# A decoder layer on one core: a new beginning ahead of the first projection chunk

## The chip, the core and the metric

The kernel runs on one core of one Trainium2 chip. A core has engines with queues of their own: TensorE (PE in the profile; its weight loads are PEld), VectorE (DVE), ScalarE (ACT), GpSimd (POOL) and SyncE (SP), which here only issues loads. Each engine works through its instructions in order and waits on semaphores for the others. The metric is the device time of one execution in microseconds (us).

## The reference, cut to what matters

A vector `c` of 2048 numbers modulates a layer on 256 tokens of width 2048. Everything is float32.

```python
c_act = jax.nn.silu(c)
mod = (c_act @ w_mod[l] + b_mod[l])[:, None, :]
sh_m, sc_m, g_m, sh_f, sc_f, g_f = jnp.split(mod, 6, axis=-1)
h = rmsnorm(x, mix_pre_w[l]) * (1 + sc_m) + sh_m
y = hybrid_mixer(h, w_in[l], ...)      # starts with proj = h @ w_in, 2048 x 6160
x = x + g_m * rmsnorm(y, mix_post_w[l])
# then the same with sh_f, sc_f, g_f around a causal ConvFFN
```

So before the first product with `w_in` there have to be: the norm of `x`, and those columns of `sh_m` and `sc_m` that belong to the first part of the width.

## The kernel before, in words

**Chunks and units.** The projection `h @ w_in` runs over the width in four chunks of 2, 4, 5 and 5 tiles of 128 (`CHUNKS`). Only the modulation of the first chunk (256 columns of `sh_m` and of `sc_m`) has to be there before TensorE starts; that of chunk 1 is summed while chunk 0 runs, and so on. A chunk has 12 units or more (`in_units`); one of chunk 0 loads a block of `w_in` of 256 x 512 (512 KB) into a `raw` buffer (`prep`), of which there are `NRAW = 6`, all shared with the rows of `w_mod`.

**High and low parts.** A weight and an activation are each split into a high part, rounded to fp32r by ScalarE (`high`: `wh`; for activations `act_high`), and a low part, the rest, by VectorE (`low`: `wl`; `act_low`). TensorE adds three products: high by high, high by low, low by high. A unit of chunk 0 is 8 triples, 24 matmuls of 256 columns.

**The modulation.** Row `j` of `w_mod` (one of 16 per partition) is scaled by `c_act[:, j]` and added to an accumulator by VectorE (`mod_steps`, `stt`). The sum over partitions is a product with ones on TensorE (`mod_columns`), of which two VectorE instructions make the columns `ash` (shift, and one plus scale times the norm's weight). Such a float32 product with two columns is two passes on TensorE.

**The beginning** (lines 957 to 979). The 16 rows are summed on VectorE. After row 3 the norm of token half 0 stands in its queue, after row 14 that of half 1: squares on ScalarE (`norm_squares`), a reduction, a square root on ScalarE, a reciprocal, and the scaling, of the first 256 columns on VectorE and of the rest on ScalarE. TensorE transposes the scaled tiles into PSUM (`turn_norm`), multiplies the accumulator with ones, and ScalarE writes the modulated tiles `hf` to SBUF, then their high parts.

**What sets the order.** The program text sets each engine's order: `drive` calls, for each unit, the preparation of later units, its own matmuls and the steps hung on it (`early`, `mid`, `late`). SP issues loads in the order of the text; each waits for a free buffer, so for the instruction that used the buffer last. In chunk 0 SP's order is two units, a pair of `w_mod` rows (two loads), a unit, a pair, two units, and so on. The fifth unit's load takes the buffer of the first unit's, which the first low part gives back.

## Time and profile before

| what | value |
|---|---|
| median of 3 runs | 1223.4 us (1222.33 to 1223.87) |
| the profiled execution | 1223.4 us, its span 1221.5 us |
| PE busy | 1174.3 us, 96% of the span |
| DVE busy | 955.2 us, 78% |
| ACT busy | 572.9 us, 47% |
| mean over the span | 263 GB/s |
| first column copy (`ash`) | 26.35 us |
| first low part of a weight | 29.62 us |
| first matmul of chunk 1 | 76.54 us |

The span runs from the first to the last instruction; the rest of the profiled execution lies around it. "Busy" counts an engine that holds an instruction, and the ends of matmuls are modelled. A wait is put down to what ended last. The granted clock of TensorE is shown as 1.00 wherever the profile holds no record of it; the first record begins at 36.4 us, so what the clock was before has to be read from the distance of the matmuls.

### The profile page before, as it was taken

How to read it: one execution, taken by the hardware profiler on the slowest of the kernel's cores; microseconds unless marked ns; L12 is line 12 of the kernel's file. 1: busy time of each engine (PE TensorE's matmuls, PEld its weight loads, DVE VectorE, ACT ScalarE, POOL GpSimd, SP SyncE). 2: the span in 40 equal slices, each digit the busy share in tenths (PEclk: the TensorE clock that was granted, in tenths of full speed). 3: DMA queues.
4: the chain of work that ended last, by engine and by line, in shares of the span. 5: the costliest groups of instructions: out<-in, count | busy, mean ns of one | idle time of the engine just before them, and what ended most of it. 6: DMA issues, size and time to landing. Idle time of an engine off the chain costs nothing.

```text
span 1221.5 us, 17082 instructions
## 1 busy us (share of the span) xinstructions
PE 1174.3 (96%) x6977; PEld 1043.0 (85%) x6977; DVE 955.2 (78%) x973; ACT 572.9 (47%) x668; POOL 31.7 (3%) x49
## 2 busy tenths in 40 slices
PE   2999999999999998999999999999999999999997
PEld 1999999989997787888888888888888888888885
DVE  5999999989998879974787979798885665444464
ACT  5553432443565437444554555454545543433441
POOL 2000020000001001000000000000000000000000
PEclk9999999999999998998999999999999999999999
DMA  9999999987599995995575776758664665555522
GB/s 306 386 390 385 311 358 394 397 284 254 190 324 347 336 343 205 383 360 169 180 268 202 250 277 208 275 206 278 239 234 150 249 246 189 207 178 201 195 81 69
DMA packets 128046, 320.73 MB, mean 263 GB/s; under 512 B 8341, under 2 KB 35685, under 8 KB 118240
## 3 DMA queue, kind: packets, MB, share of 16 engines
q1 hardware_dynamic: 125360, 312.63, 71.9%
q0 software_dynamic: 2320, 6.94, 1.6%
q8 instruction: 55, 0.90, 0.3%
q14 instruction: 23, 0.19, 0.0%
q10 hardware_dynamic: 288, 0.07, 0.0%
HBM read 315.42 MB, written 4.19 MB: 262 GB/s over the span
## 4 chain that ended last, share of the span: by engine, by line
PE 54%; DVE 0%; ACT 0%; DVEq 0%; issue 0%; ACTq 0%
PE ps L874 22%; PE ps L876 11%; PE ps L733 7%; PE ps L734 7%; PE ps L732 7%; PE ps L285 0%; DVE big L137 0%; PE ps L348 0%; PE ps L308 0%; PE ps L309 0%; ACT junk L335 0%; DVE big L727 0%; DVEq L1234 0%; DVE big L799 0%; ACT rz L321 0%
## 5 line engine op out<-in xcount | busy, mean ns | idle before, releaser
L141 ACT CAST wh<-raw 128x2048 fp32r<-128x2048 f32 (+3 forms) x202 | 366.2, 1816 | 500.2 <-PE ps L874 163.5
L146 DVE TENSOR_TENSOR wl<-raw,wh 128x2048 fp32r<-128x2048 f32 (+3 forms) x202 | 437.7, 2168 | 137.1 <-ACT wh L141 137.1
L874 PE MATMUL ps<-big,wh 128*128 128x512 f32 x1400 | 490.2, 394 | 0.0
L876 PE MATMUL ps<-big,wl 128*128 128x256 f32 x1400 | 393.3, 281 | 0.0
L874 PEld LDWEIGHTS ps<-big,wh 128*128 128x128 f32 x1400 | 263.4, 188 | 59.3
L876 PEld LDWEIGHTS ps<-big,wl 128*128 128x128 f32 x1400 | 265.8, 190 | 0.0
L479 PE MATMUL ps<-big,wl 128*128 128x256 f32 x733 | 210.7, 287 | 4.6 <-DVE wl L146 4.6
L477 PE MATMUL ps<-big,wh 128*128 128x256 f32 x733 | 211.9, 289 | 0.2 <-ACT wh L141 0.2
L478 PE MATMUL ps<-big,wh 128*128 128x256 f32 x733 | 209.9, 286 | 0.0
L137 DVE SCALAR_TENSOR_TENSOR macc<-raw,c_act,macc 128x2048 f32<-128x2048 f32 (+1 forms) x96 | 199.4, 2077 | 3.7 <-DMA raw<-in_w_mod_dram 3.6
L733 PE MATMUL ps<-wl,big 128*128 128x512 f32 x456 | 177.8, 390 | 3.6 <-DVE wl L146 3.6
L732 PE MATMUL ps<-wh,big 128*128 128x512 f32 x456 | 177.9, 390 | 0.0
L734 PE MATMUL ps<-wh,big 128*128 128x512 f32 x456 | 177.5, 389 | 0.0
L479 PEld LDWEIGHTS ps<-big,wl 128*128 128x128 f32 x733 | 143.1, 195 | 5.8 <-DVE wl L146 5.7
L477 PEld LDWEIGHTS ps<-big,wh 128*128 128x128 f32 x733 | 143.4, 196 | 2.7 <-PE ps L423 1.3
L478 PEld LDWEIGHTS ps<-big,wh 128*128 128x128 f32 x733 | 143.3, 196 | 0.1
L733 PEld LDWEIGHTS ps<-wl,big 128*128 128x128 f32 x456 | 85.6, 188 | 22.4 <-DVE wl L146 4.8
L732 PEld LDWEIGHTS ps<-wh,big 128*128 128x128 f32 x456 | 85.6, 188 | 17.8
L734 PEld LDWEIGHTS ps<-wh,big 128*128 128x128 f32 x456 | 85.6, 188 | 17.6
L137 DVE SCALAR_TENSOR_TENSOR big<-big,fcw,big 128x254 f32<-128x254 f32 (+1 forms) x176 | 72.2, 479 | 0.0
L799 DVE TENSOR_TENSOR big<-big,ps 128x256 f32<-128x256 f32 x88 | 31.1, 416 | 43.5 <-ACT big L797 43.5
L819 ACT ACTIVATE big<-big,fcw 128x256 f32<-128x256 f32 x88 | 37.8, 512 | 14.1 <-DVE big L810 14.1
(183 smaller groups left out, 686.9 us busy)
## 6 DMA issues: line engine op xcount, KB each, us to landing
raw<-in_w_up_dram SPq DMA_DIRECT2D x88, 1024.0 KB, 5.3
raw<-in_w_mod_dram SPq DMA_DIRECT2D x64, 1024.0 KB, 7.1
raw<-in_w_down_dram SPq DMA_DIRECT2D x44, 1024.0 KB, 4.8
raw<-in_w_in_dram SPq DMA_DIRECT2D x24, 960.0 KB, 8.3
raw<-in_w_mod_dram SPq DMA_DIRECT2D x32, 640.0 KB, 7.8
raw<-in_w_out_dram SPq DMA_DIRECT2D x16, 1024.0 KB, 7.0
raw<-in_w_in_dram SPq DMA_DIRECT2D x12, 1024.0 KB, 8.0
raw<-in_w_mod_dram SPq DMA_DIRECT2D x22, 512.0 KB, 6.7
```

Of the source, the lines that this page charges most:

```text
L137: nc.vector.scalar_tensor_tensor(o, a, s, b, op0=op0, op1=op1)
L141: nc.scalar.copy(hi, raw)
L146: nc.vector.tensor_sub(lo, raw, hi.bitcast(F32))
L477: nc.tensor.matmul(ps, w[0][:, kk, cs], ht[:, k % 2, 0, :], start=st, stop=False)
L478: nc.tensor.matmul(ps, w[0][:, kk, cs], ht[:, k % 2, 1, :], start=False, stop=False)
L479: nc.tensor.matmul(ps, w[1][:, kk, cs], ht[:, k % 2, 0, :], start=False, stop=sp)
L732: nc.tensor.matmul(ps, a[:, i, 0, ts_], w[0][:, kk, ns], start=st, stop=False)
L733: nc.tensor.matmul(ps, a[:, i, 0, ts_], w[1][:, kk, ns], start=False, stop=False)
L734: nc.tensor.matmul(ps, a[:, i, 1, ts_], w[0][:, kk, ns], start=False, stop=sp)
L819: nc.scalar.activation(st["c"][:, o, :], st["u"][o], AF.Copy, scale=fcw[:, 2, ch + o:ch + o + 1])
L874: nc.tensor.matmul(pss[o], wh[:, kk, cs], h2[k // 2][:, k % 2, :, :], start=(first and kk == 0), stop=False)
L876: nc.tensor.matmul(pss[o][:, 1, :], wl[:, kk, cs], h2[k // 2][:, k % 2, 0, :], start=False, stop=(last and kk == 3))
```

## The change

Six things are changed, all in the beginning.

- Twelve of the first chunk's 16 rows are summed on VectorE as before. The last four (12 to 15) are loaded into `big` slots and multiplied on TensorE with two columns of `c_act` (`first_products`): four float32 products a row, added in PSUM to the four products of ones with the accumulator. `c_act` gets two columns of zeros at its end, so that row 15 has a second column.
- The loads of the second half of `x` move ahead of rows 8 to 11. The norm of half 0 stands after row 5 in VectorE's queue, that of half 1 after row 9; the squares of half 0 are issued ahead of all rows.
- TensorE gets 16 and later 8 products of ones, 128 x 128 by 128 x 512 (`keep_busy`), whose result nothing reads.
- The high part of the first chunk's activations is written by ScalarE straight from PSUM, while VectorE writes `hf` from PSUM (`at_once`).
- The first unit runs its products in three passes (high by high, low weight by high, high by low), and the chunk's product with `alr_w` and its copy come behind it.
- The small loads move: the identity and the first bias stand first on POOL's queue, `alr_w` behind the first two units on SP's, and the casts of ones go from ScalarE to VectorE.

TensorE's queue from the start to the first unit (`ident`: transposes; `sv_r`: small vectors; `ones`: the sum of an accumulator; `alr_w`: gate rank; `wh`, `wl`: weights of the unit). Before:

```order
L209 MATMUL ps_184<-ident,sv_r 128x58
L348 MATMUL ps_187<-ident,big_109 128x128 x2
L348 MATMUL ps_187<-ident,big_149 128x128 x2
L285 MATMUL ps_193<-ones,big_102 128x2 x4
L423 MATMUL ps_204<-big_99,alr_w 16x256 x2
L477 MATMUL ps_232<-big_202,wh_211 128x256
L478 MATMUL ps_232<-big_202,wh_211 128x256
L479 MATMUL ps_232<-big_202,wl_213 128x256
```

The same place in the changed kernel:

```order
L229 MATMUL ps_182<-ident,sv_r 128x58
L368 MATMUL ps_185<-ident,big_111 128x128 x2
L217 MATMUL ps_188<-big_88,ones_r 128x512 x16
L1040 MATMUL ps_206<-c_act,big_125 128x2 x8
L1040 MATMUL ps_206<-ones,big_79 128x2 x4
L217 MATMUL ps_219<-big_88,ones_r 128x512 x8
L368 MATMUL ps_185<-ident,big_118 128x128 x2
L1040 MATMUL ps_206<-c_act,big_128 128x2 x8
L510 MATMUL ps_270<-big_244,wh_240 128x256 x2
```

Between the first transposes and the sum now stand 16 products of ones and the eight of rows 12 and 13; the second transposes stand behind eight more of ones, and the eight products of rows 14 and 15 are the last before the columns.

VectorE's queue from the accumulator's bias to the scaling of half 0 (`n_...`: sums and reciprocals of the norm; `c_act`: a row's step). Before:

```order
L187 TENSOR_TENSOR big_102<-big_102,big_103 1x512
L319 TENSOR_REDUCE n_12_130<-n_7_121 128x1
L326 RECIPROCAL n_13_132<-n_13_132 128x1
L967 TENSOR_SCALAR big_109<-big_109,n_13_132 128x256
L137 SCALAR_TENSOR_TENSOR big_102<-raw_138,c_act,big_102 128x512 x4
```

And now:

```order
L201 TENSOR_TENSOR big_79<-big_79,big_80 1x512
L136 SCALAR_TENSOR_TENSOR big_79<-raw_115,c_act,big_79 128x512 x2
L339 TENSOR_REDUCE n_19_151<-n_14_135 128x1
L346 RECIPROCAL n_20_153<-n_20_153 128x1
L1008 TENSOR_SCALAR big_111<-big_111,n_20_153 128x256
L136 SCALAR_TENSOR_TENSOR big_79<-raw_115,c_act,big_79 128x512 x2
```

Rows 4 and 5 now stand ahead of the norm's reduction.

VectorE's queue from the columns (`ash`) to the third low part of a weight. Before:

```order
L288 COPY ash_192<-ps_193 128x2
L137 SCALAR_TENSOR_TENSOR ash_192<-ps_193,sv 128x2
L367 TENSOR_TENSOR big_202<-big_99,big_202 128x2x256
L431 COPY alr<-ps_204 16x256
L146 TENSOR_TENSOR wl_213<-raw_209,wh_211 128x1024
L137 SCALAR_TENSOR_TENSOR big_219<-raw_222,c_act,big_219 128x1024
L146 TENSOR_TENSOR wl_230<-raw_215,wh_217 128x1024
```

And now:

```order
L1052 COPY ash_205<-ps_206 128x2
L136 SCALAR_TENSOR_TENSOR ash_205<-ps_206,sv 128x2
L440 TENSOR_SCALAR big_105<-ps_185,ash_205 128x256 x2
L387 TENSOR_TENSOR big_244<-big_105,big_244 128x2x256
L145 TENSOR_TENSOR wl_250<-raw_238,wh_240 128x1024
L136 SCALAR_TENSOR_TENSOR big_257<-raw_260,c_act,big_257 128x1024
L145 TENSOR_TENSOR wl_268<-raw_252,wh_254 128x1024
L136 SCALAR_TENSOR_TENSOR big_257<-raw_260,c_act,big_257 128x1024
L469 COPY alr<-ps_296 16x256
```

Two instructions that read PSUM are new ahead of the activations' low part, and the copy `alr` went behind the second low part.

The diff, cut to its core:

```diff
--- before.py
+++ after.py
@@ -35,8 +35,8 @@
 LWS = 1
 ORD = (0, 5, 1, 6, 2, 7, 3, 8, 4, 9, 10)
 NBIG = 20
-XLD = (0, 8)
-NLD = (3, 14)
+XLD = (0, 4)
+NLD = (5, 9)
 GATE = (18, 19, 20, 21)
 SILU = (17, 18)
 CONV = (9, 12, 13, 15)
@@ -49,6 +49,8 @@
 NHI = 3
 NLO = 3
 NHF = 3
+ROWS = 12
+BUSY = (16, 8)
...
@@ -70,9 +72,6 @@
 def drive(units):
     due = {}
     n = len(units)
-    units[0].prep()
-    units[0].low()
-    units[1].prep()
     for i, u in enumerate(units):
         for f in u.early:
             f()
@@ -149,13 +148,14 @@
 
     c_sb = col(KT, "c_sb")
     nc.scalar.dma_start(c_sb, c.rearrange("b (p j) -> p (b j)", j=KT))
-    c_act = col(KT, "c_act")
-    nc.scalar.activation(c_act, c_sb, AF.Silu)
+    c_act = col(KT + 2, "c_act")
+    nc.vector.memset(c_act, 0.0)
+    nc.scalar.activation(c_act[:, :KT], c_sb, AF.Silu)
 
...
+    W0 = CHUNKS[0] * P
+    first_acc = slot([P, 2, W0])
+    first_b = slot([1, 2, W0])
+    first_rows = {}
+
+    def first_load(j, m, tile):
+        r = tile([P, m, 2, W0])
+        for s in range(2):
+            nc.sync.dma_start(r[:, :, s, :], w_mod_v[:, j:j + m, s, 0:W0])
+        for i in range(m):
+            first_rows[j + i] = r[:, i, :, :]
+
+    def first_step(j):
+
+        cj = c_act[:, j:j + 1]
+        if j == 0:
+            nc.vector.tensor_scalar_mul(first_acc, first_rows[j], cj)
+        else:
+            stt(first_acc, first_rows[j], cj, first_acc)
+        if j == 3:
+            nc.vector.tensor_add(first_acc[0:1], first_acc[0:1], first_b)
 
     ident = col(P, "ident")
-    nc.scalar.dma_start(ident, ident_in)
+    nc.gpsimd.dma_start(ident, ident_in)
+    nc.gpsimd.dma_start(first_b, b_mod_v[:, 0:2, 0:W0])
     ones = col(P, "ones")
     nc.gpsimd.memset(ones, 1.0)
     ones_r = col(P, "ones_r", F32R)
-    nc.scalar.copy(ones_r, ones)
+    nc.vector.tensor_copy(ones_r, ones)
+    busy_r = slot([P, 4, P], F32R)
+    nc.vector.tensor_copy(busy_r, ones.unsqueeze(1).to_broadcast([P, 4, P]))
+
+    def keep_busy(n):
+
+        ps = bank([P, 4, P])
+        for i in range(n):
+            nc.tensor.matmul(ps, ones_r, busy_r, start=i == 0, stop=i == n - 1)
+
...
@@ -407,10 +427,28 @@
         k0, k1 = bounds[ci], bounds[ci + 1]
         kept = []
 
+        def at_once():
+
+            n = CHUNKS[0]
+            for kts in pairs(k0, k1):
+                ps, hf = early.pop(0), hf0[:, kts[0]:kts[-1] + 1, :]
+                d = hts[kts[0] // 2] = slot([P, 2, 2, T], F32R)
+                ab = [(ash[:, n + k:n + k + 1], ash[:, k:k + 1]) for k in kts]
+                for i, (a, b) in enumerate(ab):
+                    nc.scalar.activation(d[:, i, 0, :], ps[:, i, :], AF.Identity, bias=b, scale=a)
+                for i, (a, b) in enumerate(ab):
+                    nc.vector.tensor_scalar(hf[:, i, :], ps[:, i, :], a, b, op0=ALU.mult, op1=ALU.add)
+                    h32.setdefault(ci, {})[kts[i]] = hf[:, i, :]
+                act_low(d, hf)
+                kept.append((kts, hf, None))
+
         def first():
+            if early:
+                at_once()
+                return
             for kts in pairs(k0, k1):
-                ps = early.pop(0) if early else turn_norm(xs, kts)
-                hf = hf0[:, kts[0]:kts[-1] + 1, :] if ci == 0 else hf_tile()
+                ps = turn_norm(xs, kts)
+                hf = hf_tile()
                 modulate(ps, kts, ash, CHUNKS[ci], k0, hf)
                 for i, k in enumerate(kts):
                     h32.setdefault(ci, {})[k] = hf[:, i, :]
@@ -445,7 +483,7 @@
             groups += [(40, 41, 42), (43, 44, 45), (46, 47)]
         banks = {}
 
-        def unit(tiles, plain):
+        def unit(tiles, plain, by_parts=False):
             m = len(tiles)
             cur = {}
 
@@ -465,6 +503,16 @@
                 for o, nt in enumerate(tiles):
                     if nt // 2 not in banks:
                         banks[nt // 2] = bank([P, 2, T])
+                if by_parts:
+                    for j, (wi, xl) in enumerate(((0, 0), (1, 0), (0, 1))):
+                        for kk in range(n):
+                            for o, nt in enumerate(tiles):
+                                nc.tensor.matmul(banks[nt // 2][:, nt % 2, :], w[wi][:, kk, o * P:(o + 1) * P],
+                                                 hts[(k0 + kk) // 2][:, (k0 + kk) % 2, xl, :],
+                                                 start=(j == 0 and kk == 0 and nt % 2 == 0),
+                                                 stop=(j == 2 and kk == n - 1 and nt % 2 == 1))
+                    return
+                for o, nt in enumerate(tiles):
                     ps = banks[nt // 2][:, nt % 2, :]
                     cs = slice(o * P, (o + 1) * P)
                     for kk in range(n):
@@ -485,7 +533,7 @@
 
             return Unit(prep, lows, mm, [fin])
 
...
-    for j, f in enumerate(steps0):
-        f()
+    def norm_rows(t, ss):
+        r = rstd_of(ss, 4, f"n1{t}")
+        e = CHUNKS[0] * P
+        nc.vector.tensor_scalar_mul(xs[t][0][:, :e], xs[t][0][:, :e], r)
+        nc.scalar.activation(xs[t][0][:, e:], xs[t][0][:, e:], AF.Copy, scale=r)
+        nc.scalar.activation(xs[t][1], xs[t][1], AF.Copy, scale=r)
+
+    for j in range(0, ROWS, 4):
+        first_load(j, 4, raw_tile)
         if j in XLD:
             load_x(XLD.index(j))
-        if j == 0:
-            load_small()
+    for j in range(ROWS, KT, 2):
+        first_load(j, 2, slot)
+    load_small()
+    chunks = [in_units(ci) for ci in range(len(CHUNKS))]
+    ss = [norm_squares(0, "n10"), None]
+    for j in range(ROWS):
+        first_step(j)
         if j in NLD:
             t = NLD.index(j)
-            r = rstd_of(norm_squares(t, f"n1{t}"), 4, f"n1{t}")
-            e = CHUNKS[0] * P
-            nc.vector.tensor_scalar_mul(xs[t][0][:, :e], xs[t][0][:, :e], r)
-            nc.scalar.activation(xs[t][0][:, e:], xs[t][0][:, e:], AF.Copy, scale=r)
-            nc.scalar.activation(xs[t][1], xs[t][1], AF.Copy, scale=r)
-    nc.sync.dma_start(alr_w, w_in[:, 6144:6160].rearrange("(k p) n -> p k n", p=P))
+            norm_rows(t, ss[t])
+            if t == 0:
+                ss[1] = norm_squares(1, "n11")
     small_columns()
     early = [turn_norm(xs, kts, None, (0,)) for kts in pairs(0, CHUNKS[0])]
+    keep_busy(BUSY[0])
+    ash = const.tile([P, 2 * CHUNKS[0]], F32, tag="ash0", name="ash0")
+    ps0 = bank([P, 2 * CHUNKS[0], 2])
+
+    def first_products(j):
+
+        n = CHUNKS[0]
+        for o in range(2 * n):
+            cs = slice((o % n) * P, (o % n + 1) * P)
+            a, r = (first_acc[:, o // n, cs], ones[:, 0:2]) if j < 0 else (first_rows[j][:, o // n, cs], c_act[:, j:j + 2])
+            nc.tensor.matmul(ps0[:, o, :], a, r, start=(j == ROWS and o == 0), stop=(j == KT - 1 and o == 2 * n - 1))
+
+    for j in range(ROWS, KT - 2):
+        first_products(j)
+    first_products(-1)
+    keep_busy(BUSY[1])
     for kts, ps in zip(pairs(0, CHUNKS[0]), early):
         turn_norm(xs, kts, ps, (1,))
-    ash, products, columns = mod_columns(accs0, CHUNKS[0], pre_c[:, :CHUNKS[0]], "ash0")
-    products()
-    columns()
-    for f in modulate_chunk(0, ash, early):
-        f()
-
-    chunks = [in_units(ci) for ci in range(len(CHUNKS))]
+    for j in range(KT - 2, KT):
+        first_products(j)
+    chunks[0][0].prep()
+    n0 = CHUNKS[0]
+    nc.vector.tensor_copy(ash[:, :n0], ps0[:, :n0, 0])
+    stt(ash[:, n0:], ps0[:, n0:, 0], 1.0, pre_c[:, :n0], ALU.add, ALU.mult)
+    first, second, third = modulate_chunk(0, ash, early)
+    first()
+    chunks[0][0].low()
+    chunks[0][1].prep()
+    nc.sync.dma_start(alr_w, w_in[:, 6144:6160].rearrange("(k p) n -> p k n", p=P))
+    chunks[0][0].mid.append(second)
+    chunks[0][0].late.append(third)
+
```

21 lines of the change are left out of this document (5 added, 16 removed).

## The prediction

> **What bounds the kernel now.** The change ends before chunk 0's second unit, so I read the stretch up to the start of chunk 1 (76.5 us), and first the stretches view: a row is a stretch, busy time of PE, PEld, DVE, ACT and POOL (instructions), granted clock, DMA share, GB/s.
>
> ```profile
> 21.80:25.10 3.30, 1.31 (x5) 0.95 (x6) 2.13 (x6) 2.09 (x3) 0.00 (x0) 1.00 0.87 246
> 30.90:36.20 5.30, 5.30 (x25) 5.30 (x26) 5.26 (x5) 1.39 (x2) 0.00 (x0) 1.00 1.05 395
> 25.10:43.40 18.30, 16.41 (x96) 14.53 (x97) 14.38 (x15) 10.37 (x16) 0.00 (x0) 1.00 1.03 378
> 43.40:61.80 18.40, 16.84 (x136) 16.27 (x136) 15.79 (x14) 10.53 (x16) 0.00 (x0) 1.00 1.05 386
> 67.10:70.50 3.40, 3.40 (x19) 3.40 (x18) 2.17 (x2) 2.78 (x3) 0.00 (x0) 0.50 1.04 391
> 76.50:137.00 60.50, 60.50 (x506) 60.46 (x506) 59.85 (x48) 22.93 (x16) 0.00 (x0) 1.00 1.03 378
> ```
>
> DMA is full from 25 us on. TensorE is solid only from 76.5 us, at 60.5/506 = 0.12 us a matmul; in 30.9 to 36.2 us it needs 5.3/25 = 0.21 for the same form. Next, who waits in chunk 0: VectorE's timeline (start, duration, instruction, in brackets its idle time before and what ended it).
>
> ```profile
> 43.49 2.60 DVE L137 SCALAR_TENSOR_TENSOR big<-raw,c_act,big 128x1024 f32<-128x1024 f32 x2 [0.68 <-DMA raw<-in_w_mod_dram]
> 48.29 1.28 DVE L137 SCALAR_TENSOR_TENSOR big<-raw,c_act,big 128x1024 f32<-128x1024 f32 x1 [1.05 <-DMA raw<-in_w_mod_dram]
> 52.31 1.28 DVE L137 SCALAR_TENSOR_TENSOR big<-raw,c_act,big 128x1024 f32<-128x1024 f32 x1 [0.41 <-DMA raw<-in_w_mod_dram]
> 57.69 2.60 DVE L137 SCALAR_TENSOR_TENSOR big<-raw,c_act,big 128x1024 f32<-128x1024 f32 x2 [0.62 <-DMA raw<-in_w_mod_dram]
> 61.78 2.60 DVE L137 SCALAR_TENSOR_TENSOR big<-raw,c_act,big 128x1024 f32<-128x1024 f32 x2 [0.36 <-DMA raw<-in_w_mod_dram]
> 64.64 1.92 PE L285 MATMUL ps<-ones,big 128*128 128x2 f32 x16 [0.28 <-DVE big L137]
> 69.36 1.55 DVE L137 SCALAR_TENSOR_TENSOR macc<-raw,c_act,macc 128x1280 f32<-128x1280 f32 x1 [1.24 <-DMA raw<-in_w_mod_dram]
> ```
>
> From 43.5 us on VectorE waits again and again for weights, and TensorE waits for VectorE's last sum at 64.64. From 52.31 to 57.69 four loads of 512 KB come, one each 1.35 us. So what ends chunk 0 is the stream of loads. Its bytes don't change: **an earlier start can't be passed on; a later one can**, if it keeps buffers (NRAW = 6) and leaves the stream empty. Is it near that? SP's wait for the fifth chunk-0 load, the issue of the load ahead and its own (the second of the first row's two), and the time from issue to landing of the load ahead, of this one, and of a 256 KB store on a quiet queue at the end:
>
> ```profile
> SPq L454 <- DVE wl L146: 5.4, 1, 5.4
> 24.88 6.34 SPq L454 DMA_DIRECT2D raw<-in_w_in_dram  x2
> 30.85 0.37 SPq L454 DMA_DIRECT2D raw<-in_w_in_dram  x1
> raw<-in_w_in_dram SPq DMA_DIRECT2D x1, 512.0 KB, 10.0
> raw<-in_w_in_dram SPq DMA_DIRECT2D x1, 512.0 KB, 5.4
> out_dram<-big SPq DMA_DIRECT2D x1, 256.0 KB, 2.6
> ```
>
> SP stood 5.4 us until the first low part `wl` gave a buffer back. The load ahead landed at 34.9, this one at 36.25, one load time (1.35) later: no gap. The store's 2.6 less 0.68 for 256 KB leaves 1.9 us before bytes move, so that issue could come up to 34.9 - 1.9 = 33.0. The margin is 2.1 us.
>
> **The change, part by part.** Rows of the timeline of the beginning, the landing time of one load under its issue, and three rows from later on for fast TensorE passes and for VectorE's reading of PSUM:
>
> ```profile
> 3.49 0.55 SPq L180 DMA_DIRECT2D raw<-in_w_mod_dram  x1
> raw<-in_w_mod_dram SPq DMA_DIRECT2D x1, 512.0 KB, 9.5
> 9.96 0.68 DVE L187 TENSOR_TENSOR big<-big,big 1x512 f32<-1x512 f32 x1
> 11.55 0.16 DVE L319 TENSOR_REDUCE n<-n 128x1 f32<-128x4 f32 x1 [0.90 <-ACT junk L335]
> 13.60 0.35 DVE L967 TENSOR_SCALAR big<-big,n 128x256 f32<-128x256 f32 x1
> 13.87 8.81 DVE L137 SCALAR_TENSOR_TENSOR big<-raw,c_act,big 128x512 f32<-128x512 f32 x11
> 14.01 0.69 PE L348 MATMUL ps<-ident,big 128*128 128x128 f32 x2 [3.06 <-DVE big L967]
> 14.44 1.13 ACT L969 ACTIVATE big<-big,n 128x1024 f32<-128x1024 f32 x1
> 17.37 0.63 ACT L335 ACTIVATE junk<-big 128x512 bf16<-128x512 f32 x1 [1.79 <-DMA big<-in_x_dram]
> 20.16 0.19 ACT L335 ACTIVATION_READ_ACCUMULATOR junk<-big 128x1 f32 x1
> 24.47 1.84 PE L285 MATMUL ps<-ones,big 128*128 128x2 f32 x8
> 26.35 0.16 DVE L288 COPY ash<-ps 128x2 f32<-128x2 f32 x1 [1.90 <-PE ps L285]
> 26.67 1.02 ACT L354 ACTIVATE big<-ps,ash 128x256 f32<-128x256 f32 x2 [1.39 <-DVE ash L137]
> 28.37 0.69 DVE L367 TENSOR_TENSOR big<-big,big 128x512 fp32r<-128x512 f32 x1 [1.80 <-ACT big L363]
> 29.62 1.20 DVE L146 TENSOR_TENSOR wl<-raw,wh 128x1024 fp32r<-128x1024 f32 x1
> 31.95 1.21 DVE L146 TENSOR_TENSOR wl<-raw,wh 128x1024 fp32r<-128x1024 f32 x1
> 70.87 1.03 PE L348 MATMUL ps<-ident,big 128*128 128x128 f32 x8
> 74.71 1.90 PE L423 MATMUL ps<-hf,alr_w 128*16 128x256 f32 x8
> L799 DVE TENSOR_TENSOR big<-big,ps 128x256 f32<-128x256 f32 x88 | 31.1, 416 | 43.5 <-ACT big L797 43.5
> ```
>
> 1. *First norm behind rows 4 and 5.* The first two rows are rows 4-7's second load: issued 3.49, landed 13.0, at the same place in the queue as before. Two rows at 8.81/11 = 0.80 end at 14.6; the norm's reduction then stands at 14.6, not 11.55: **+3.05**. The two transposes that released TensorE (14.01 to 14.5) come at 17.1 and end at 17.6.
>
> 2. *Sixteen products of ones.* 256 columns cost 0.21 slow, 0.12 fast; 512 twice that. TensorE ran 5.3 us slow (30.9 to 36.2) before it was fast. I take the same: the 13 products that start within 5.3 us slow, 3 fast, 6.2 us, end 23.8. Bounds: all fast 3.8, all slow 6.8.
>
> 3. *Rows 12 and 13.* A row is 4 products of two passes. A pass costs 0.11 fast (the x16 row) and 0.21 slow (the x8 row). Fast after the ones: 16 passes 1.8, end 25.6. The 8 passes of ones by the sum 0.9, end 26.5; the sum is there: the second norm on ScalarE starts at 18.6 (15.57 + 3.05), its squares take 20.35 - 17.37 = 3.0, VectorE scales at 22.5 and ends rows 10 and 11 at 24.4. That is all behind TensorE. VectorE's four rows fewer (3.2 us) buy nothing, since TensorE's queue comes last.
>
> 4. *Eight more ones* 1.9, *two transposes* 0.2 (eight take 1.03), *rows 14 and 15* 1.8: end 30.4. **The column copy stands at 30.5, not 26.35: +4.15.** Landing isn't the limit: their loads are in by 21.9 before (the last of the eleven-row run starts there). Bounds: 28.1 with all ones fast, 34 and more with passes slow.
>
> 5. *High parts from PSUM.* Before, copy to `wl` took 29.62 - 26.35 = 3.27. Now ScalarE's two take 0.32 + 1.02 = 1.35 from the copy, VectorE's two 128x256 (0.42 each) lie beside them, the low part 0.69: 2.05. A saving of **1.2**. The alr products and copy leave VectorE's path ahead of `wl`; the copy (0.41) comes back four instructions later, and TensorE's 4 passes (half of 1.90) behind unit 0, where TensorE has slack. Net: `wl` starts at 30.5 + 2.05 = 32.55, **2.9 later**.
>
> 6. *What that does to the stream.* `wl` ends at 33.75, the fifth load issues at 33.8, bytes move at 35.7 instead of 34.9: 0.8 lost. The next pair waits for the second `wl` (31.95 + 1.21 = 33.15 before, 36.1 now), moves at 38.0 where the stream is free at 37.05: 0.95 lost. The load behind it issues at 37.3 under cover of the pair. Sum: **1.75 late**, and nothing left of it is made good, for the stream stays full to the end of chunk 0. VectorE's own lateness (3.3 by then) is covered by its idle 0.68 + 1.05 + 0.41 + 0.62 + 0.36 = 3.1.
>
> 7. *At no cost:* alr_w behind two loads moves its slow spot (246 GB/s in 21.8 to 25.1), not its bytes; ident on POOL's queue; rows 12-15 in `big` slots; VectorE's casts of ones before the first row lands; unit 0 in three passes, whose slow clock before no longer counts because loads set the pace. Price if alr_w's spot vanished: 3.3 x (1 - 246/386) = 1.2 gained. The stretch 43.49 to 48.29 took 4.8 for three loads (4.05 elsewhere); nothing shown causes it, I keep it; without it 0.75 comes back.
>
> Sum: 1223.4 (the profiled execution; span 1221.5, the rest lies around it; also the median) + 1.7 = **1225.1**. Chunk 1 is solid TensorE, so the shift goes on to the end.
>
> One rule speaks against the change. The Trainium skill, "TensorE: Matmul & The Clock Gate", Part 1, says that the clock is granted by free-running windows of some 3.4 us, and that one quiet window halves it. The 5.3 us slow start and the 3.4 us at 0.50 in the table agree with that. By its window alone the sixteen ones would have 3.4 to 6.8 us slow, which as an estimate puts the copy at 29.6 to 31.1.
>
> **Rivals.**
>
> *The clock falls back between the two blocks of ones* (slower). At 67.1 us it stood at 0.50 for 3.4 us, right after the 16 two-column passes of 64.64; the change puts 24 such passes in a row. Then the eight ones cost 3.4, transposes 0.5, the last 16 passes 3.4: copy at up to 34.0, `wl` done at 37.25, the fifth load moves at 39.2: 4.3 + 0.95 = 5.2 late; with half of it slow 3.4. I take +4.2: **1227.6**. It decides once the copy is later than about 31.3. Against it: eight ones lie there, and the phase of the clock varies. This is what that rule of the Trainium skill would make of it.
>
> *The stream swallows everything.* If the ones run fast early, the copy is at 28.1, `wl` done at 31.3, inside the margin: 0 lost, or -0.75 without the slow stretch: **1223.0**. For it: the stream alone ends chunk 0. Against: item 1 needs no guess.
>
> *Faster.* The stream loses its slow stretch and alr_w's spot (0.75 + 1.2), and the half clock at 67.1 to 70.5 (3.4/2 = 1.7 of matmul work, of which ScalarE and VectorE hide most) goes: up to -2.9, **1220.5**. For it: TensorE is warm earlier. Against: the bytes are the same, and VectorE's 1.24 wait for weights at 69.36 ends that stage too.
>
> **How the numbers follow.** Forecast 0.5, clock 0.2, swallowed 0.18, faster 0.12. A measurement of this kernel can't tell less than 0.2% (2.4 us) from nothing. The forecast (+1.7) lies within, with a tail above of 0.08; swallowed lies within; the clock rival is slower; the last is faster, 0.11 of it. So faster 0.11, same 0.62, slower 0.27. Range: 1221.6 (below the swallowed case, most of the slow spots gone) to 1228.0 (the clock rival's middle with some room); 0.1 lies below, 0.09 above.
>
> **What would show it.** Norm's reduction at 14.6; column copy at 30.5; first `wl` at 32.5; SP's fifth chunk-0 load at 33.8 and a dip of GB/s behind 34 us; VectorE without a wait for weights until about 52; products of chunk 1 at 66.4 instead of 64.64; TensorE's ones 0.43 apart, then 0.24. Wrong if the copy is earlier than 28, if loads land earlier than 1.35 us apart, or if the start of chunk 1 (76.5) moves by more than its products do.

## The result and the profile after

The changed kernel takes 1235.6 us (median of 9 executions, 1228.1 to 1238.9) against 1223.9 for the kernel before, run beside it (9, 1222.3 to 1231.8): ratio 1.0061, 95% interval 1.0032 to 1.0090. It is slower, by less than 1% but clear of the noise, and above the top of the predicted range (1228.0). The profiled execution took 1229.2 us, its span 1227.1 (before 1223.4 and 1221.5). One thing is needed to read these medians, about 12 us apart: executions of either kernel run the stretch from about 600 to 970 us at one of two paces, some 7 us apart, and by their times six of the nine of the kernel before ran at the faster pace (median 1223.5) and only three of the nine of the changed one (1229.2), so I compare beginnings by an event ahead of that stretch, the products that make chunk 1's columns.

VectorE's timeline of the changed kernel, from the norm to the third low part of a weight, a choice of rows (start, duration, instruction, in brackets the idle time before it and what ended it):

```profile
14.80 0.15 DVE L339 TENSOR_REDUCE n<-n 128x1 f32<-128x4 f32 x1
29.39 0.16 DVE L1052 COPY ash<-ps 128x2 f32<-128x2 f32 x1 [5.01 <-PE ps L1040]
30.76 1.00 DVE L440 TENSOR_SCALAR big<-ps,ash 128x256 f32<-128x256 f32 x2 [1.15 <-ACT big L438]
32.41 1.22 DVE L145 TENSOR_TENSOR wl<-raw,wh 128x1024 fp32r<-128x1024 f32 x1
38.54 0.41 DVE L469 COPY alr<-ps 16x256 f32<-16x256 f32 x1 [1.39 <-PE ps L461]
40.07 1.21 DVE L145 TENSOR_TENSOR wl<-raw,wh 128x1024 fp32r<-128x1024 f32 x1
```

The norm, the column copy and the first `wl` stand near where they were predicted (14.6, 30.5, 32.55). Two waits were not in the sum: 1.15 us until ScalarE has finished its reads of PSUM, and 1.39 us for the alr products. The third `wl`, at 35.59 before, is 4.5 us late where the first is 2.8 late. TensorE's timeline, a choice of rows, says why:

```profile
17.60 5.30 PE L217 MATMUL ps<-big,ones_r 128*128 128x512 f32 x16
22.74 1.84 PE L1040 MATMUL ps<-c_act,big 128*128 128x2 f32 x16
25.34 2.12 PE L217 MATMUL ps<-big,ones_r 128*128 128x512 f32 x8
27.51 1.84 PE L1040 MATMUL ps<-c_act,big 128*128 128x2 f32 x16
33.68 2.07 PE L510 MATMUL ps<-big,wl 128*128 128x256 f32 x8 [1.61 <-DVE wl L145]
35.55 1.91 PE L510 MATMUL ps<-big,wh 128*128 128x256 f32 x8
37.39 1.11 PE L461 MATMUL ps<-big,alr_w 128*16 128x256 f32 x4
69.75 1.92 PE L305 MATMUL ps<-ones,big 128*128 128x2 f32 x16 [0.17 <-ACT wh L140]
```

From 20.5 us on TensorE runs fast, the passes before 29.4 at 0.11 us apiece. At 30.7 the clock falls to half: the first unit's last 16 products start 0.23 us apart. The alr products wait behind them, their copy waits for them, and the third `wl` waits behind the copy. The last row is the products of chunk 1's columns: 64.64 before, 69.75 now, +5.1. So the loss is complete before 70 us; behind it VectorE stays 4.7 to 5.9 us late, and 5.45 us from 600 us on. The prediction had 66.4.

Now the stream of loads: the stretch from the landing of the load ahead of the fifth to that of the 19th load after, first of the kernel before, then of the changed one (busy times, granted clock, DMA share, GB/s):

```profile
34.90:61.70 26.80, 25.24 (x200) 24.67 (x200) 23.66 (x20) 16.14 (x24) 0.00 (x0) 1.00 1.04 383
```

```profile
35.40:66.80 31.40, 27.45 (x209) 25.70 (x209) 26.13 (x23) 16.13 (x24) 0.00 (x0) 0.97 0.96 335
35.40:44.00 8.60, 8.60 (x60) 7.66 (x60) 7.21 (x8) 4.06 (x6) 0.00 (x0) 0.87 0.85 287
```

The same 19 loads take 4.6 us more; nearly the whole loss is here, and nearly half of it in the first 9 us. In a stretch as long the kernel before moved 371 GB/s:

```profile
34.90:44.00 9.10, 9.10 (x72) 9.10 (x72) 8.39 (x8) 6.09 (x9) 0.00 (x0) 1.00 1.03 371
```

Why loads came late is in SP's timeline:

```profile
33.69 0.37 SPq L492 DMA_DIRECT2D raw<-in_w_in_dram  x1
35.98 0.88 SPq L176 DMA_DIRECT2D raw<-in_w_mod_dram  x2
41.30 0.88 SPq L176 DMA_DIRECT2D raw<-in_w_mod_dram  x2
```

and in its waits from 20 to 66 us (total, times, longest):

```profile
SPq L176 <- DVE wl L145: 13.7, 6, 3.8
SPq L492 <- DVE wl L145: 7.4, 2, 6.7
```

Each waits for a low part `wl` to give its buffer back. From issue to landing the loads issued at 33.69, 35.98 and 41.30 then took (last number):

```profile
raw<-in_w_in_dram SPq DMA_DIRECT2D x1, 512.0 KB, 4.1
raw<-in_w_mod_dram SPq DMA_DIRECT2D x1, 512.0 KB, 4.5
raw<-in_w_mod_dram SPq DMA_DIRECT2D x1, 512.0 KB, 3.7
```

These loads, issued onto a queue that had run low, needed 3.7 to 4.5 us, not the 1.9 + 1.35 = 3.25 that I took from a store. And VectorE, which was to catch up in its idle time, still waits for weights:

```profile
52.71 1.28 DVE L136 SCALAR_TENSOR_TENSOR big<-raw,c_act,big 128x1024 f32<-128x1024 f32 x1 [1.79 <-DMA raw<-in_w_mod_dram]
57.56 1.28 DVE L136 SCALAR_TENSOR_TENSOR big<-raw,c_act,big 128x1024 f32<-128x1024 f32 x1 [1.23 <-DMA raw<-in_w_mod_dram]
62.89 2.61 DVE L136 SCALAR_TENSOR_TENSOR big<-raw,c_act,big 128x1024 f32<-128x1024 f32 x2 [0.58 <-DMA raw<-in_w_mod_dram]
66.88 2.60 DVE L136 SCALAR_TENSOR_TENSOR big<-raw,c_act,big 128x1024 f32<-128x1024 f32 x2 [0.25 <-DMA raw<-in_w_mod_dram]
```

These are 3.85 us of idle time, more than the 3.1 before.

### The profile page after: what moved, and what is told of

Same layout as the page of the kernel before. It is cut to its first block, busy times and chain, and to the rows that moved or that the text cites. A ratio compares the mean times of both kernels' runs of the same rounds, so it can differ in the third digit from the quotient of the medians.

```text
span 1227.1 us, 17192 instructions
## 1 busy us (share of the span) xinstructions
PE 1179.5 (96%) x7033; PEld 1048.0 (85%) x7033; DVE 953.1 (78%) x974; ACT 571.8 (47%) x666; POOL 32.3 (3%) x50
## 4 chain that ended last, share of the span: by engine, by line
PE 53%; DVE 0%; ACT 0%; DVEq 0%; issue 0%; ACTq 0%
PE ps L922 22%; PE ps L924 11%; PE ps L782 7%; PE ps L780 7%; PE ps L781 6%; PE ps L305 0%; DVE big L136 0%; PE ps L368 0%; PE ps L328 0%; PE ps L329 0%; ACT junk L355 0%; DVE big L775 0%; DVEq L1314 0%; DVE big L847 0%; ACT rz L341 0%
## 5 line engine op out<-in xcount | busy, mean ns | idle before, releaser
L922 PEld LDWEIGHTS ps<-big,wh 128*128 128x128 f32 x1400 | 263.0, 188 | 59.2
L525 PE MATMUL ps<-big,wh 128*128 128x256 f32 x725 | 207.7, 286 | 0.0
L526 PE MATMUL ps<-big,wh 128*128 128x256 f32 x725 | 205.8, 284 | 0.0
L525 PEld LDWEIGHTS ps<-big,wh 128*128 128x128 f32 x725 | 139.7, 193 | 2.1 <-PE ps L461 1.3
L526 PEld LDWEIGHTS ps<-big,wh 128*128 128x128 f32 x725 | 139.8, 193 | 0.1
```

Source lines behind the costliest of these rows:

```text
L525: nc.tensor.matmul(ps, w[0][:, kk, cs], ht[:, k % 2, 0, :], start=st, stop=False)
L526: nc.tensor.matmul(ps, w[0][:, kk, cs], ht[:, k % 2, 1, :], start=False, stop=False)
L922: nc.tensor.matmul(pss[o], wh[:, kk, cs], h2[k // 2][:, k % 2, :, :], start=(first and kk == 0), stop=False)
```

## The experiments

The theory: VectorE gives the raw buffers back late, the stream runs dry, and both stay late together. Its rivals: that the order of loads, the rows in other buffers or the three passes cost the time; that the late columns alone explain it; that the stream loses time by chance. All profiles in one table, worked out from issue and landing of each load: a load's lead is the time from its issue to the landing of the load before it; "pair" is the pair of rows loaded next after the fifth load. The last column is the whole time against the kernel before run beside it, with its 95% interval; it holds the two paces too. The expectations speak of chunk 1's first matmul; in all runs but one it follows the products by 10.4 us, or by 11.9 where the clock is down for 3.4 us at about 70 us, so I read the products.

| kernel | column copy | third `wl` | lead, fifth load | lead, pair | 19 loads take | products of chunk 1's columns | time to before |
|---|---|---|---|---|---|---|---|
| before | 26.35 | 35.59 | 4.05 | 3.08 | 26.75 | 64.64 | - |
| before, again | 26.60 | 35.84 | 4.37 | 3.39 | 26.77 | 65.22 | 1.0010 (0.9992 to 1.0029) |
| before, third | 27.26 | 36.50 | 4.29 | 3.32 | 26.89 | 65.93 | 1.0008 (0.9993 to 1.0023) |
| before, ten rows | 24.20 | 35.39 | 6.70 | 4.48 | 26.76 | 65.16 | 1.0011 (0.9986 to 1.0035) |
| before, early ones | 27.21 | 36.45 | 4.04 | 3.03 | 29.51 | 68.25 | 1.0012 (0.9990 to 1.0034) |
| before, early ones, again | 26.64 | 36.13 | 5.02 | 4.05 | 26.98 | 66.13 | 1.0003 (0.9988 to 1.0017) |
| before, 4 ones ahead of the columns | 28.35 | 37.59 | 2.95 | 2.32 | 29.34 | 68.12 | 1.0022 (1.0011 to 1.0033) |
| before, 7 ones | 28.41 | 37.36 | 2.18 | 1.63 | 29.24 | 67.04 | 1.0014 (1.0004 to 1.0025) |
| before, two buffers | 26.66 | 35.91 | 9.63 | 10.02 | 26.49 | 64.92 | 1.0018 (0.9968 to 1.0067) |
| before, two buffers, 7 ones | 28.91 | 38.15 | 9.92 | 10.45 | 28.77 | 67.64 | 1.0020 (0.9996 to 1.0044) |
| changed | 29.39 | 40.07 | 1.67 | 1.77 | 31.40 | 69.75 | 1.0061 (1.0032 to 1.0090) |
| changed, again | 29.37 | 40.20 | 2.10 | 1.62 | 30.84 | 69.60 | 1.0052 (1.0028 to 1.0077) |
| changed, alr copy later | 28.97 | 37.97 | 2.61 | 1.63 | 28.93 | 67.80 | 1.0075 (1.0059 to 1.0091) |
| changed, rows on VectorE | 27.98 | 38.88 | 2.59 | 1.90 | 29.94 | 67.75 | 1.0095 (1.0080 to 1.0110) |
| changed, no ones | 29.99 | 40.93 | 1.85 | 1.64 | 30.90 | 70.02 | 1.0040 (0.9991 to 1.0089) |
| changed, norm early | 31.90 | 42.79 | -0.28 | 1.81 | 33.26 | 72.19 | 1.0063 (1.0018 to 1.0108) |
| changed, ones once, alr later | 30.82 | 39.82 | 1.27 | 2.48 | 29.50 | 68.88 | 1.0016 (1.0005 to 1.0027) |
| changed, two buffers | 34.42 | 45.39 | 8.09 | 8.92 | 36.60 | 75.24 | 1.0042 (0.9996 to 1.0089) |

### Both kernels again

> The changed kernel once more, for a second profile of it and five more rounds. If the clock's phase in the ones is set by the program, the half-clock stretch begins at 30.7 us again and the column copy stands at 29.4; if it is chance, the copy lies anywhere from 29 to 34.5 (it was at 31.9 and 34.4 with the same ones in two variants) and chunk 1's start moves with the third wl, one for one.

> The kernel before once more, for a second profile. Its fifth chunk-0 load is issued 4.1 us ahead of the landing of the load before it, the next pair 3.07 us ahead, and nothing was lost there in the first profile. If the loss in the changed kernel comes from lateness alone, this profile repeats the first: the 19 loads from the fifth on take 26.8 us, chunk 1 begins at 76.5 (less the difference of the starts) within 0.4. If the stream has slow spots by chance, it differs by 1 to 3 us.

> The kernel before a third time: by lateness alone the 19 loads from the fifth on take 26.8 us once more and chunk 1 begins at 76.5 within 0.4; by chance slow spots it differs by 1 to 3 us.

The changed kernel repeats: half clock from 31.0, copy at 29.37, products at 69.60; ratio 1.0052 (1.0028 to 1.0077). The kernel before repeats too: 26.75, 26.77 and 26.89 us for the 19 loads, its products at 64.64 to 65.93 as its first loads come earlier or later. So against the mean of three (65.26) the change costs 4.4 us. The loss is there in both profiles of the changed kernel and in none of the three of the kernel before.

### The delay alone

```diff
+    keep_busy(7)
     products()
     columns()
```

(and four in place of seven in the other run)

> The kernel before, with seven products of ones (512 columns) put on TensorE ahead of the products that make the first modulation's columns; nothing else changes. It delays the column copy by about 3.0 us (7 x 0.43 at the slow clock). Theory (lateness of VectorE's queue, passed on through the raw buffers): first wl +3.0, third wl +3.0, chunk 1's first matmul (76.54 before) +2 to +3.5. By the prediction's own step 6: 0.9 + 0.95, so about +1.8. Rival (the order of loads in the changed kernel slows the stream, not the late copy): +0 to +0.5, since the loads here stand in the old order.

> As the other, with four products of ones: the column copy about 1.7 us later. By the margin of 2.1 us that the prediction read, the stream is not left empty and chunk 1's first matmul stays within 0.4 us of 76.54. If the margin is smaller than read, or VectorE's lateness counts by itself, it is +1 to +2.

Rows of the timelines of VectorE and TensorE with seven ones, and the stretch of the same 19 loads:

```profile
28.41 0.16 DVE L295 COPY ash<-ps 128x2 f32<-128x2 f32 x1 [4.00 <-PE ps L292]
37.36 1.22 DVE L146 TENSOR_TENSOR wl<-raw,wh 128x1024 fp32r<-128x1024 f32 x1
...
67.04 1.92 PE L292 MATMUL ps<-ones,big 128*128 128x2 f32 x16 [0.17 <-ACT big L406]
```

```profile
34.80:64.10 29.30, 26.95 (x209) 26.35 (x209) 25.47 (x22) 16.14 (x24) 0.00 (x0) 0.95 1.01 359
```

The ones warmed TensorE (the clock came up at 27.7 us), so seven delayed the copy by 2.1 us and not 3.0; with four it is 2.0 later, 0.7 of it from a later landing of the first loads. Nothing else is changed, and the third `wl` is 1.8 to 2.0 late. The stream takes 2.5 us more, the products are 2.4 and 3.5 us later than in the first profile of the kernel before (1.8 and 2.9 later than the mean of three). By the margin I had read, 2.1 us, the second case should have cost nothing. The whole time agrees (1.0014 and 1.0022). The mechanism holds without the change's other parts; the margin doesn't. A lead isn't the whole account either: with four ones the pair had the longer lead (2.32 against 1.63) and yet took 6.2 us from issue to landing, against 4.1 with seven. No run shows why.

### The alr copy one unit later

```diff
-    chunks[0][0].late.append(third)
+    chunks[0][1].late.append(third)
```

> The changed kernel, with VectorE's copy of the alr products put behind unit 1 in place of unit 0. Theory: VectorE's 1.39 us wait for TensorE in front of the third wl is part of the loss: first wl as in the changed kernel (+2.8), third wl +2.8 in place of +4.48, chunk 1's first matmul about +3.3 in place of +5.1. Rival (the loss is all in the late column copy): third wl earlier, chunk 1 still +4.5 to +5.1.

```profile
31.98 1.22 DVE L145 TENSOR_TENSOR wl<-raw,wh 128x1024 fp32r<-128x1024 f32 x1
37.97 1.22 DVE L145 TENSOR_TENSOR wl<-raw,wh 128x1024 fp32r<-128x1024 f32 x1
40.30 0.41 DVE L469 COPY alr<-ps 16x256 f32<-16x256 f32 x1
...
67.80 1.92 PE L305 MATMUL ps<-ones,big 128*128 128x2 f32 x16 [0.23 <-ACT big L419]
```

The copy no longer waits, the third `wl` is 2.4 late in place of 4.5, and the products come 1.95 us earlier than in the changed kernel (67.80 against 69.75); the 19 loads take 28.93 in place of 31.40. So 1.5 to 2 of the five microseconds are this one copy: 0.4 of the 1.95 belongs to a column copy that came earlier (28.97 against 29.39), and from the first to the third `wl` it is 5.99 us in place of 7.66. (The whole time is no measure of it: the profiled execution also lost 6.8 us behind 600 us.)

### Without ones, and with the rows on VectorE

```diff
-BUSY = (16, 8)
+BUSY = (0, 0)
```

> The changed kernel without the 24 products of ones. Theory: the passes then run at half clock (0.21 us) and the copy comes at about 30, as late as with the ones; time as the changed kernel, ratio 1.005 to 1.008. Rival (the 7.4 us of ones in TensorE's queue are the cost): copy about 24 to 26 and time as before, ratio 1.000.

Here the clock stays low until 38.7 us, rows 12 and 13 take 3.54 us and the copy stands at 29.99, only 0.6 later than with 24 ones; the products come at 70.02 against 69.75 and 69.60. The ones cost about what they save.

```diff
-NLD = (5, 9)
-ROWS = 12
-BUSY = (16, 8)
+NLD = (3, 9)
+ROWS = 16
+BUSY = (0, 0)
```

(and the sum as one group of four products of ones, behind the second transposes)

> The changed kernel with all sixteen rows summed on VectorE again, no products of ones, and the norms at rows 3 and 9; loads, high parts from PSUM, three passes in unit 0 and the alr products behind unit 0 as in the changed kernel. Theory: the column copy comes at about 27 (26.35 before, 29.4 changed), first wl about +0.3, third wl about +2 (TensorE is slow in unit 0, VectorE waits 1.6 us for the alr products), chunk 1's first matmul +0 to +1. Rival (the order of loads slows the stream): chunk 1 +4 to +5 although the copy is early.

Here the order of loads, the high parts from PSUM, the three passes and the alr copy are those of the change, and the copy comes at 27.98 (27 expected: VectorE waits 1.68 us for rows at 18.83). The alr copy waits 1.60 us, the third `wl` is 3.3 late, the products are at 67.75: 2.0 better than the changed kernel, no better than with the alr copy moved. The rival that blames the order of loads expected 4 to 5 us in spite of an early copy, the theory 0 to 1; it is 2.5 (against the mean of the kernel before), as the late third `wl` would have it. Neither figure was hit. No run takes the order of loads or the three passes by itself, so a share of theirs isn't excluded; the delay alone, which loses in the old order, shows only that they aren't needed for a loss.

### The clock in the ones

```diff
-NLD = (5, 9)
+NLD = (3, 9)
```

> The changed kernel with the first norm's reduction back behind row 3 (NLD 3, 9). Theory (the stream of loads runs empty, because the column copy at 29.39 us against 26.35 gives buffers back late): TensorE's queue starts 3 us earlier, but then waits for the sum (about 23 us), so the copy moves only to about 28.2, the first wl to 31.2, the fifth chunk-0 load to 32.4, near the margin: 0 to 1 us of stream lost, time 0 to 2 us over before (ratio 1.000 to 1.002). Rival (TensorE's added work and half clock cost the time, wherever the norm stands): as the changed kernel, ratio about 1.006.

```diff
-BUSY = (16, 8)
+BUSY = (16, 0)
```

(and the alr copy one unit later)

> The changed kernel without the second block of eight ones, and with the copy of the alr products one unit later. Column copy at about 27.4 (29.4 less 2.0), first wl at 30.4, third wl +0.8 against the kernel before. Theory (chunk 1 follows the third wl one for one): chunk 1's first matmul +0.5 to +1.5 in place of +5.1, and the whole time within 0.2 % of before where both run at one pace later on. Rival (the order of loads, rows in other buffers, three passes): still +3 or more.

In both the column copy missed (31.90 for 28.2, 30.82 for 27.4), for one reason. TensorE without the second block of ones, and the stretches around it with the granted clock as the third number from the right:

```profile
17.98 6.22 PE L219 MATMUL ps<-big,ones_r 128*128 128x512 f32 x16
24.04 1.84 PE L1042 MATMUL ps<-c_act,big 128*128 128x2 f32 x16
27.37 3.41 PE L1042 MATMUL ps<-c_act,big 128*128 128x2 f32 x16
```

```profile
22.90:26.30 3.40, 3.40 (x27) 3.18 (x26) 1.83 (x4) 2.84 (x3) 0.00 (x0) 1.00 0.82 174
24.00:27.40 3.40, 3.40 (x28) 3.36 (x27) 0.76 (x2) 1.74 (x2) 0.00 (x0) 0.84 0.77 214
27.40:30.80 3.40, 3.39 (x17) 3.30 (x16) 0.00 (x0) 0.00 (x0) 0.00 (x0) 0.50 0.86 271
```

The clock comes up at 22.9 and falls at 26.3, while TensorE is busy all the time (3.40 of 3.40 us), from 24.2 on with two-column passes, and rows 14 and 15 take 3.41 in place of 1.84. With the norm early it came up at 20.0 and fell at 23.4, for 17 us. So the rival on the clock is real. It strikes where the ones end soon after the clock has come up: 1.3 us after here, 1.0 with the norm early; in the changed kernel it came up at 20.5, the ones ran on for 2.4 us, and it held until 30.7. The Trainium skill, "TensorE: Matmul & The Clock Gate", Part 1, lets the clock fall after an idle window of some 3.4 us; the length agrees (22.9 to 26.3), the condition doesn't: TensorE was busy through this window by the profile, if mostly with two-column passes. With the alr copy moved, the kernel with 16 ones has its products at 68.88 in spite of this, 0.9 earlier than the changed kernel. Its rival's figure, +3 or more, did come (4.2 against the first profile of the kernel before, 3.6 against the mean); as the copy itself was 3.4 us later than planned, the run decides nothing on the order of loads.

### More buffers

```diff
-                r = raw_tile([P, n, m * P])
+                r = (slot if ci == 0 and tiles[0] in (24, 28) else raw_tile)([P, n, m * P])
```

> The kernel before with the same two big slots. Theory: its stream was full already (margin 2.1 us), so nothing changes: ratio 0.999 to 1.000. Rival (buffers bound the kernel before as well): 1 us or more faster.

> The changed kernel with the first two units of chunk 0 loaded into big slots, so that the fifth unit's load and the next pair find raw buffers free and wait for no low part. Nothing else moves. Theory: SP issues the fifth load before 28 us, no dip of GB/s at 34 us, the last pair of chunk 1's rows lands at about 62 instead of 66.8, copy still at 29.4; time 0 to 1 us over before (ratio 1.000 to 1.001). Rival (TensorE's work, half clock, or the alr copy in VectorE's queue): as the changed kernel, ratio about 1.006.

> The kernel before with the seven products of ones that made it 1.8 us late at chunk 1, and the first two weight loads of chunk 0 in two buffers more, so that two loads more can be under way. If the late return of raw buffers leaves the stream empty, two loads (2.7 us) of cover swallow the 1.77 us: third wl +1.8, chunk 1 within +0.5. If VectorE's own queue is the limit, chunk 1 is +1.8 again.

In the kernel before, two loads more under way gain nothing (26.49, products at 64.92): the stream is full already. With the delay of seven ones they don't save it either, and the products are 2.4 us behind the mean, more than either reading expected: the fifth load and the first pair land on time, but the 19 loads take 28.77. The loads after the two extra ones wait for the same late `wl`: the next pair has a lead of 1.78 and lands 0.65 us late. The rest are two gaps, of 1.3 us at 47.20 and 1.0 at 63.29, at loads with leads of about 4, of the kind that is taken up below. In the changed kernel the clock happened to fall at 26.1, the copy came at 34.42, and the products went to 75.24: worse, for the reason of the section above. A few loads of cover move the dry stretch; here they didn't remove it.

### An earlier start

```diff
+            if first and j >= 10:
+                return
```

> The kernel before with rows 10 to 15 left out of the first modulation's sum (their loads are still made). VectorE's sum and the second norm end earlier, the column copy comes about 2.5 us earlier; the first wl follows by up to 1.8 (then the weights' own load at 26.67 and its cast bound it). By the prediction an earlier start can't be passed on: chunk 1's first matmul at 76.5 within 0.4. If VectorE's queue sets the pace one for one: 74.7 to 75.5.

```diff
     early = [turn_norm(xs, kts, None, (0,)) for kts in pairs(0, CHUNKS[0])]
+    keep_busy(20)
```

> The kernel before with twenty products of ones on TensorE behind the first two transposes, in its idle time from 14.7 to 23.7 us, and nothing else. They end by 23.4 at the latest, so they delay nothing; with TensorE fast the eight passes of the columns take 1.0 in place of 1.84 and the alr products 1.0 in place of 1.9: column copy 0.8 earlier, first wl 0.8 to 1.6 earlier. If lateness and earliness of VectorE's queue both pass on one for one, chunk 1's first matmul comes 0.8 to 1.6 earlier; by the prediction (the stream of loads ends chunk 0, so an earlier start can't be passed on) it stays at 76.5 within 0.3.

> The kernel before with twenty early products of ones, again. In its first profile everything up to the first wl was 0.8 late because the loads of x were, VectorE was not late against the stream, and yet the stream lost 2.8 us more from the next pair on. If that was chance: chunk 1 now near 76.5 to 77.5. If it belongs to the program: again about +3 against its own start.

With rows 10 to 15 left out of the sum the copy is 2.15 us earlier and the first `wl` too:

```profile
24.20 0.16 DVE L290 COPY ash<-ps 128x2 f32<-128x2 f32 x1 [2.15 <-PE ps L287]
27.48 1.20 DVE L146 TENSOR_TENSOR wl<-raw,wh 128x1024 fp32r<-128x1024 f32 x1
29.84 1.28 DVE L137 SCALAR_TENSOR_TENSOR big<-raw,c_act,big 128x1024 f32<-128x1024 f32 x1 [1.16 <-DMA raw<-in_w_mod_dram]
...
65.16 1.92 PE L287 MATMUL ps<-ones,big 128*128 128x2 f32 x16 [0.23 <-ACT big L401]
```

VectorE then waits for its next weights, and the products stay: 65.16 against 64.64 to 65.93. (Chunk 1's first matmul comes at 75.56, 1 us earlier than in the first profile, since the clock isn't down at 70 us; in the third profile of the kernel before it isn't either.) An earlier start isn't passed on, as predicted. So by this run a quicker beginning alone has nothing to gain, and none of the runs beats the kernel before.

The early ones missed their aim: the clock fell at 24.9, so the columns were no faster. Their two profiles differ: in one the pair was issued 3.03 us ahead and the 19 loads took 29.51; in the other 4.05 ahead, and 26.98. The kernel before has 3.08 to 3.39 and lost nothing. Either it stands very near to an edge, or the lead isn't all that decides; one profile doesn't tell. Of the 2.8 us half, 1.4, is lost at the pair itself, the rest at two later loads that had been issued 4 and 6 us ahead.

## Why the prediction was wrong, step by step

**What ends chunk 0.** Right: the stream of loads, which passes on a later start and not an earlier one (ten rows; the delay alone).

**Items 1 to 4, the column copy.** The norm at 14.80 (14.6) and the transposes at 17.26 (17.1) held. The sixteen ones took 5.30 (6.2), as TensorE was fast 2.9 us after their start and not 5.3; everything behind them came that much earlier, and the copy at 29.39 (30.5): +3.04 and not +4.15.

**Item 5, high parts from PSUM.** Wrong: copy to `wl` took 3.02, not 2.05, so 0.25 was saved and not 1.2. VectorE's two reads don't lie beside ScalarE's: they wait 1.15 us until both are done, as the row at 30.76 shows. The Trainium skill has the rule that I had missed, "PSUM — Partial Sum Buffer", "PSUM bank collisions raise a hardware error": the compiler's scheduler adds a dependency between instructions of two engines that touch the same bank in the same 32 partitions, reads against reads included. The trace agrees with it (the 1.15 us); no run tried it by itself. This error and the last one cancel by luck: the first `wl` stands at 32.41, with 32.55 predicted.

**The alr copy in item 5.** Wrong, and the largest single step. I counted the copy's own 0.41 us and TensorE's slack; I didn't ask what it waits for. It stands in VectorE's queue ahead of the third `wl` and waits for products that now stand behind a unit at half clock. From the first to the third `wl` it is 7.66 us, where it was 5.97: 1.7 us that had no place in the sum. The run that moves the copy gives 1.95 us back, 0.4 of it from an earlier column copy.

**Item 6, the stream.** Right in kind, mis-sized. The issues were predicted well (33.69 for 33.8, 35.98 for 36.1). But the margin of 2.1 us rested on a store's 1.9 us before bytes move. Loads on a queue that had run low took 3.7 to 4.5 from issue to landing (up to 6.2 in the variants), 2.4 to 3.2 before the bytes of 1.35 us; over the variants the fifth load landed on time with a lead of 4, and late by 0.4 us with 2.2, 1.0 with 1.67, 2.1 with 1.27, 3.0 with -0.28, if with scatter (on time with 2.61, 0.35 late with 2.95). So the first two stalls cost 1.0 and 1.4 us (the landings are 2.39 and 2.74 apart), not 0.8 and 0.95. The next pair, behind the alr copy, was issued 4.5 us later than before and cost another 0.5.

**"Nothing of it is made good", and item 7's slow stretch.** The stretch that I kept at 0.75 grew: the load that landed 2.08 us after the one before it (at 45.45) in the kernel before landed 2.97 after it (49.28), and a second such gap of 2.5 us appeared at 57.44. Together with the three stalls, less 0.4 that the kernel before lost at the third of them, that makes 4.6 us for 19 loads, where I had 1.75. Without extra buffers, every kernel whose pair had a lead of 3.03 us or less lost 2 us or more in the 19 loads, partly in gaps of this kind where loads had been issued long before; all from 3.08 us on lost nothing.

What holds those loads up was tested by no run, but the traces show a companion of some of them. Beside the queue of the loads the profile lists a DMA queue of kind `instruction`. Here is a load of 16 KB on it in the kernel before (42.6 to 42.8 us) and one in the changed kernel (54.8 to 55.0): packets, MB, and their time as a share of the 16 DMA engines over 0.2 us.

```profile
q8 instruction: 1, 0.02, 32.5%
```

```profile
q8 instruction: 1, 0.02, 34.0%
```

So each took 1.0 to 1.1 us of engine time. The landing at 45.45 comes 2.7 us behind the first, that at 57.44 2.5 us behind the second. In all three profiles of the kernel before a landing 0.7 to 1.0 us late follows the first such load by 2.2 to 2.8 us, so this is a candidate for the slow stretch of item 7, for which I had found no cause; in the changed kernel there are two in the 19 loads that could count, at 37.28 inside the second stall and at 54.91, and in the kernel before one, as its second comes at 60.78, with 0.9 us to go. Not every one has such an effect (without ones none follows that at 57.79), and at the landing at 49.28 there is none. Ahead of that one the DMA engines were busy but slow, compared with a full stretch (the last two numbers are DMA share and GB/s):

```profile
45.30:48.30 3.00, 3.00 (x27) 3.00 (x27) 3.00 (x3) 1.10 (x3) 0.00 (x0) 1.00 0.89 264
52.00:54.90 2.90, 2.10 (x18) 1.89 (x16) 2.19 (x2) 1.23 (x2) 0.00 (x0) 1.00 1.05 388
```

The cause of these gaps, 2 of the 4.6 us, stays open.

**VectorE's cover.** Wrong: the idle 3.1 us were waits for loads, and when buffers and loads form a ring, the loads come later by what VectorE is late. The waits grew to 3.85.

**The rivals.** The time of the clock rival (1227.6) was the nearest to the profiled 1229.2, but that is luck: its mechanism didn't strike between the blocks of ones, though it did behind the first block in three variants. The half clock came one step later, in the first unit, where the alr products, and so their copy, waited behind it. "Swallowed" and "faster" fell with the margin.

**The time.** +5.8 us in the profiled pair, of which 5.1 at the products of chunk 1's columns, against +1.7 predicted. Of the difference of 3.4 at the products, 1.5 to 2 is the alr copy and its wait (by its run), the rest a stream that loses more than its late issues explain.

## What to carry to other kernels

Where loads and the work that frees their buffers form a ring that is full, as here, an earlier start gains nothing and a later one is paid, so look first for the margin: take it from issue to landing of the same kind of load on a queue that has run low, for each load that is issued late, and allow for scatter. An instruction that is moved in an in-order queue costs what it then waits for, and so does everything behind it; its own duration says little. And before counting two engines' reads of one PSUM tile as parallel, look for a row in which they overlap.

## What was not expected of the hardware

**Two paces at a clock of 1.00.** From about 600 to 970 us some executions run TensorE 2% slower. Here are the kernel before at the fast pace and the changed kernel with the alr copy later at the slow one: the 512-column products from 640 to 700 us, with their mean ns as the second number behind the bar, and that stretch.

```profile
L874 PE MATMUL ps<-big,wh 128*128 128x512 f32 x174 | 60.4, 391 | 0.0
```

```profile
640.00:700.00 60.00, 60.00 (x348) 52.91 (x347) 52.80 (x72) 30.53 (x38) 0.00 (x0) 1.00 0.65 224
```

```profile
L922 PE MATMUL ps<-big,wh 128*128 128x512 f32 x170 | 60.1, 399 | 0.0
```

```profile
640.00:700.00 60.00, 60.00 (x341) 52.00 (x341) 49.29 (x67) 29.90 (x37) 0.00 (x0) 1.00 0.66 223
```

348 matmuls in 60 us against 341, both at a granted clock of 1.00, and some 7 us over the stage. Variants of both kernels show either; in one series 26 of 35 executions of the kernel before took 1228 to 1235 us, in two others 2 of 54. Whether the changed program takes the slow pace more often isn't shown: in the series with the alr copy moved and with the rows on VectorE all eight executions of these two took 1232 us or more, and none of 19 of the kernel before; without the second block of ones 11 of 12 took 1225 to 1228.3. Nothing in the profiles tells what sets it.

**The clock's phase repeats.** Two profiles of the changed kernel have half clock from 30.7 and from 31.0, for 6.8 us each, which speaks for the program setting it; two profiles don't prove it. It is touchy: with the ones 0.4 us later (17.98 against 17.60) the clock came up 2.4 us later (22.9 against 20.5), and the copy 1.4 us later, though eight ones fewer stood ahead of it.
